# Token-major projections of a two-layer encoder: one matmul over 128 rows, or two over 64 rows into two PSUM banks

## The chip, the cores and the metric

The kernel runs on one core of a Trainium2 chip. The metric is the device time of one execution in microseconds, lower is better; the time before is the median of three runs.

## The reference

Two residual layers over 256 tokens of 2048 features, all in float32. Layer 0 mixes tokens by grouped-query attention (16 query heads, 4 key heads, RMS-norm of each head, rotary positions), layer 1 by a recurrent block (input projection, convolution of width 4, two gated linear recurrences, a GeLU gate, output projection). Each layer then has a feed-forward part with 5632 hidden features:

```python
def swiglu(h, w_gate, w_up, w_down):
    return (jax.nn.silu(h @ w_gate) * (h @ w_up)) @ w_down

for i in range(DEPTH):
    h = rms_norm(x, norm_mix[i])
    mix = attention_mixer(h, ...) if i % N_MIXERS == 0 else recurrent_mixer(h, ...)
    x = x + mix
    x = x + swiglu(rms_norm(x, norm_ffn[i]), ffn_w_gate[i], ffn_w_up[i], ffn_w_down[i])
```

Nearly all arithmetic is in the products with weight matrices: query, key and value (2048 x 3072), attention output, recurrent input (2048 x 4096) and output, and gate, up and down of each feed-forward part.

## The kernel before

**Precision.** TensorE multiplies in fp32r, a float32 format of lower precision. Each float32 operand is kept as a pair: `hi`, its value rounded to fp32r, and `lo`, the rest. A product takes three matmuls: hi with hi, hi with lo, lo with hi.

**Weights.** Weights come from HBM in pieces of 512 KB ("halves", `raw`, 128 partitions x 1024), in a fixed order. `load_half` (lines 106 to 118) issues the DMA on SP's queue, casts the piece to `hi` on ACT (L116) and takes the rest `lo` on DVE (L117). `raw`, `hi` and `lo` have five buffers each, so loads and casts run ahead of the matmuls by up to five pieces.

**Two kinds of projection.** The feature-major ones (`project`, `project_sum`, `project_two`; L201 and L231 to L233) hold weights as the stationary operand and stream 256 tokens (or 512 columns, hi and lo of the tokens side by side). The token-major ones, `project_tokens` (lines 211 to 228, matmuls at L223), hold 128 tokens of an activation as the stationary operand (128 features on the rows of the array, 128 tokens on its columns) and stream 512 output features of the weights. A call makes one group of 512 output features for all 256 tokens: two sums of 128 tokens x 512 in two PSUM banks, over 12 or 16 feature tiles `k`, with three matmuls for each `k` and half of the tokens `a`. In the last piece the order is such that the sum of the first 128 tokens is done six matmuls before the other.

Token-major are the attention's output projection, the recurrent output projection, and gate, up and down of both feed-forward parts. `output` (lines 376 to 390) calls `project_tokens` for four column groups and adds each sum to the residual `x_tok` on DVE (L384); in the last feed-forward part it also stores the result (L386), the last column group in two halves. `ffn` (line 635) works through the hidden features in parts of 12, 16 and 16 tiles of 128. A unit of four tiles is a gate call, whose sums go through SiLU on ACT into `fg`, and an up call, whose sums are multiplied with `fg` on DVE into `fu` (L641); `turned` (line 344) transposes it on DVE and ACT into four feature-major tiles, and L645 and L646 make the operand pair `act` from each. Then the down projection of that part runs over its tiles, the newest four last.

**Norms.** After each column group of `output`, `Norm.add` takes the sum of squares of the residual and makes operand tiles `xg` of it. For the recurrent block `Norm.spread` puts the tokens' scale on a diagonal (`ndg`, L330) and spreads it with a small matmul (L336) that the rest of the input projection waits for.

**PSUM.** Two pools of four banks each: `ps_a` for the sums of projections (tag `acc`) and `ps_m` for everything small in attention, recurrence and norms (tag `pm`). A call of `project_tokens` takes two banks of `ps_a`, so the next call can start while the sums of the last are read.

**Order.** The order on PE is that of the program. Work of attention heads and recurrence blocks is put between the projections' matmuls by `later(delay, fn)` and `step()`: a function is called after so many steps. So the last heads' transposes, scores and values are issued inside the first call of the attention's output projection. On the other engines the framework orders the instructions.

Of the kernel before, what the change touches and what calls it, by code (L numbers as in the profile page):

```python
# [12 lines left out]
F32 = mybir.dt.float32  # L13
F32R = mybir.dt.float32r
AF = mybir.ActivationFunctionType
ALU = mybir.AluOpType
AX = mybir.AxisListType

P = 128
# [10 lines left out]
WIDE = 512  # L30
# [39 lines left out]
def trunk(ctx, tc, w, out):  # L70
    nc = tc.nc
    act, dve, pool, pe, sync = nc.scalar, nc.vector, nc.gpsimd, nc.tensor, nc.sync
# [7 lines left out]
    ps_m = ctx.enter_context(tc.tile_pool(name="ps_m", bufs=4, space=bass.MemoryType.PSUM))  # L80
# [5 lines left out]
    def nm(s):  # L86
        uid[0] += 1
        return f"{s}_{uid[0]}"
# [61 lines left out]
    def half():  # L150
        n = taken[0]
        taken[0] += 1
        if n == 0:
            load_x(0, 2)
            scale_x(0)
            return load_half(*order[n], 4, partial(load_x, 2, 2))
        if n == 1:
            scale_x(1)
            return load_half(*order[n], 2)
        if n < KT // 2:  # L160
            if n % 2 == 0:
                load_x(2 * n, 4)
            if n < KT // 2 - 1:
                scale_x(n)
        if n == KT // 2 - 2:
            scale_x(n + 1)
            load_tables()
        if n == KT // 2 + 2:
            tiles = load_half(*order[n])
            token_squares(1)  # L170
            return tiles
        return load_half(*order[n])
# [8 lines left out]
    def step():  # L181
        clock[0] += 1
        due = [i for i, (t, _) in enumerate(waiting) if t <= clock[0]]
        if due:
            waiting.pop(due[0])[1]()

    def flush():
        while waiting:
            waiting.pop(0)[1]()

    def new_acc():
        return ps_a.tile([P, 2 * S], F32, tag="acc", name=nm("acc"))
# [16 lines left out]


    def project_tokens(xs, ready=0, close=None):
        accs = [new_acc() for _ in range(2)]
        for k0 in range(0, len(xs), 2):
            if close is not None and k0 == ready:
                flush()
                close()
            half()
            hi, lo = (t.rearrange("p (k c) f -> p k (c f)", k=2) for t in newest["tiles"])
            end = k0 + 2 == len(xs)
            for k, a in ((0, 0), (1, 0), (0, 1), (1, 1)) if end else ((0, 0), (0, 1), (1, 0), (1, 1)):  # L220
                xh, xl = (xs[k0 + k][:, o + a * P : o + (a + 1) * P] for o in (0, S))
                for n, (x, wt) in enumerate(((xh, hi), (xh, lo), (xl, hi))):
                    pe.matmul(  # L223
                        accs[a], x, wt[:, k, :], start=(k0 + k == 0 and n == 0), stop=(end and k == 1 and n == 2)
                    )
                step()
                step()
        return accs

    def three(o, hi, lo, x, start, stop):  # L230
        pe.matmul(o, hi, x[:, :S], start=start, stop=False)  # L231
# [8 lines left out]
    def project_sum(xs):  # L240
        bank = new_acc()
        for k0 in range(0, len(xs), HALF):
            sums(bank[:, :S], half(), xs, k0)
        return bank[:, :S], bank[:, S:]


    def project_two(xs, late):
        banks = [new_acc() for _ in range(2)]
        for t in banks:
            sums(t[:, :S], half(), xs, 0)  # L250
        rest = [half() for _ in range(2)]
        n = len(xs) - HALF - late
        for t, wt in zip(banks, rest):
            sums(t[:, :S], wt[:n], xs, HALF)
        for t, wt in zip(banks, rest):
            sums(t[:, :S], wt[n:], xs, HALF + n)
            yield t[:, :S], t[:, S:]
# [101 lines left out]
    fp = []  # L359
# [16 lines left out]
    def output(xs, norm=None, end=False, ready=0, close=None):  # L376
        for c in range(NCOL):
            accs = project_tokens(xs, ready, None if c else close)
            for a, acc in enumerate(accs):
                n = 2 if end and c == NCOL - 1 else 1  # L380
                for i in range(n):
                    sl = slice(i * WIDE // n, (i + 1) * WIDE // n)
                    y = x_tok[:, a, c, sl]
                    dve.tensor_tensor(y, y, acc[:, sl], ALU.add)  # L384
                    if end:
                        sync.dma_start(out=out[:, a, c, sl], in_=y)  # L386
            if norm is not None:
                norm.add(c)
        if norm is not None:
            norm.finish()  # L390
# [70 lines left out]
    for chunk in KEY_TILES:  # L461
        wt = half()
# [172 lines left out]
    def ffn(norm, nxt):  # L635
        def unit():
            g, u = (fp[0].tile([P, 2, WIDE], F32, tag=t, name=nm(t), bufs=1) for t in ("fg", "fu"))
            for a, acc in enumerate(project_tokens(norm.xs)):
                table_act(g[:, a, :], acc, AF.Silu, scale=norm.rt[:, a : a + 1])
            for a, acc in enumerate(project_tokens(norm.xs)):  # L640
                dve.scalar_tensor_tensor(u[:, a, :], acc, norm.rt[:, a : a + 1], g[:, a, :], ALU.mult, ALU.mult)  # L641
            for f in turned(u):
                h = act_tile()
                hi, lo = (h[:, o : o + S].rearrange("p (q t) -> p q t", t=32) for o in (0, S))
                act.copy(hi, f)  # L645
                dve.tensor_tensor(lo, f, hi.bitcast(F32), ALU.subtract)  # L646
                yield h

        for p, n in enumerate(PARTS):
            hid = [h for _ in range(n // FOUR) for h in unit()]  # L650
            last = p == len(PARTS) - 1
            if last and nxt is not None:
                ln_exp_tables()
            output(hid, nxt if last else None, last and nxt is None)
# [108 lines left out]
    for b in range(-1, NBLK):  # L763
# [9 lines left out]
        if nxt:  # L773
            accs = (project_sum(nr.xs) for _ in range(2)) if blk else project_two(nr.xs, FOUR)
# [101 lines left out]
```

## Time and profile before

| | before |
|---|---|
| median of 3 runs (lowest to highest) | 2036.44 us (2036.38 to 2036.95) |
| span of the profiled execution, first to last instruction | 2034.8 us |
| PE busy / weight loads busy | 2021.0 / 1722.5 us |
| DVE / ACT / POOL busy | 1311.9 / 1157.2 / 168.6 us |
| matmuls | 10124 |
| moved by DMA | 386.02 MB, mean 190 GB/s |
| mean granted TensorE clock | 0.998 |

The table of times gives no separate time for the profiled execution: its span is 1.6 us under the median of the runs. In rows of the profile a group is given as line, engine, operation, result <- operands, shape, count, then busy time in us and mean duration of one in ns, then the idle time of the engine just ahead of these instructions and what ended it. PEld is the weight load of a matmul, which the profile lists apart from PE. Matmuls are pipelined, so their durations overlap and the step from start to start is the cost of one.

### The profile page before, as it was taken

How to read it: one execution, taken by the hardware profiler on the slowest of the kernel's cores; microseconds unless marked ns; L12 is line 12 of the kernel's file. 1: busy time of each engine (PE TensorE's matmuls, PEld its weight loads, DVE VectorE, ACT ScalarE, POOL GpSimd, SP SyncE). 2: the span in 40 equal slices, each digit the busy share in tenths (PEclk: the TensorE clock that was granted, in tenths of full speed). 3: DMA queues.
4: the chain of work that ended last, by engine and by line, in shares of the span. 5: the costliest groups of instructions: out<-in, count | busy, mean ns of one | idle time of the engine just before them, and what ended most of it. 6: DMA issues, size and time to landing. Idle time of an engine off the chain costs nothing.

```text
span 2034.8 us, 27445 instructions
## 1 busy us (share of the span) xinstructions
PE 2021.0 (99%) x10124; PEld 1722.5 (85%) x10124; DVE 1311.9 (64%) x1899; ACT 1157.2 (57%) x1776; POOL 168.6 (8%) x213
## 2 busy tenths in 40 slices
PE   9999999999999999999899999999999999999999
PEld 8898888888888888888799998888888888888887
DVE  7998765654665445667778987765555556555553
ACT  7665755544555345556689987755435554355442
POOL 1563000000000000000134330000000000000000
PEclk9999999999999999999999999999999999999999
DMA  8444565665666656666556555566666666666664
GB/s 319 157 135 145 186 202 193 186 203 191 187 197 197 195 195 193 186 199 196 188 165 188 187 157 194 180 205 197 190 194 195 193 190 196 196 189 195 197 202 129
DMA packets 108998, 386.02 MB, mean 190 GB/s; under 512 B 12224, under 2 KB 12992, under 8 KB 108736
## 3 DMA queue, kind: packets, MB, share of 16 engines
q1 hardware_dynamic: 108720, 384.26, 59.7%
q8 instruction: 79, 1.29, 0.3%
q14 instruction: 55, 0.45, 0.1%
q10 hardware_dynamic: 144, 0.02, 0.0%
HBM read 382.13 MB, written 2.10 MB: 189 GB/s over the span
## 4 chain that ended last, share of the span: by engine, by line
PE 54%; issue 40%; DVE 2%; DMA 2%; ACT 1%; POOL 0%; SPq 0%; DVEq 0%; POOLq 0%
PE acc L223 40%; PE acc L201 3%; PE acc L231 3%; PE acc L232 3%; PE acc L233 3%; PE pm L232 1%; PE pm L233 1%; PE pm L231 1%; DVE lo L117 1%; DMA x_tok<-in_xt_dram 1%; DMA graw<-in_w_gates_dram 0%; DMA raw<-in_w_k_dram 0%; PE pm L576 0%; DMA raw<-in_w_qv_dram 0%; ACT hi L116 0%
## 5 line engine op out<-in xcount | busy, mean ns | idle before, releaser
L117 DVE TENSOR_TENSOR lo<-raw,hi 128x1024 fp32r<-128x1024 f32 (+1 forms) x708 | 868.7, 1230 | 665.5 <-ACT hi L116 657.1
L116 ACT CAST hi<-raw 128x1024 fp32r<-128x1024 f32 (+1 forms) x708 | 739.4, 1047 | 751.7 <-PE acc L223 744.0
L223 PE MATMUL acc<-hi,xg 128*128 128x512 f32 x2816 | 867.8, 389 | 0.0
L223 PEld LDWEIGHTS acc<-hi,xg 128*128 128x128 f32 x2816 | 528.6, 188 | 109.6
L223 PE MATMUL acc<-hi,act 128*128 128x512 f32 x1920 | 594.2, 389 | 0.0
L223 PE MATMUL acc<-lo,xg 128*128 128x512 f32 x1408 | 547.7, 389 | 0.0
L223 PEld LDWEIGHTS acc<-hi,act 128*128 128x128 f32 x1920 | 360.4, 188 | 74.4
L223 PE MATMUL acc<-lo,act 128*128 128x512 f32 x960 | 373.5, 389 | 0.0
L223 PEld LDWEIGHTS acc<-lo,xg 128*128 128x128 f32 x1408 | 264.3, 188 | 54.9
L223 PEld LDWEIGHTS acc<-lo,act 128*128 128x128 f32 x960 | 180.2, 188 | 37.1
L231 PE MATMUL acc<-xg,hi 128*128 128x256 f32 x512 | 145.0, 283 | 0.0
L232 PE MATMUL acc<-xg,hi 128*128 128x256 f32 x512 | 145.0, 283 | 0.0
L233 PE MATMUL acc<-xg,lo 128*128 128x256 f32 x512 | 144.7, 283 | 0.0
L201 PE MATMUL acc<-xg,hi 128*128 128x512 f32 x384 | 125.8, 396 | 0.2 <-ACT hi L116 0.2
L354 ACT COPY tf<-tb 32x256 f32<-32x256 f32 x272 | 109.8, 404 | 3.7 <-DVE tb L348 0.2
L231 PEld LDWEIGHTS acc<-xg,hi 128*128 128x128 f32 x512 | 98.3, 192 | 0.0
L232 PEld LDWEIGHTS acc<-xg,hi 128*128 128x128 f32 x512 | 98.2, 192 | 0.1
L233 PEld LDWEIGHTS acc<-xg,lo 128*128 128x128 f32 x512 | 98.2, 192 | 0.0
L201 PEld LDWEIGHTS acc<-xg,lo 128*128 128x128 f32 x384 | 71.8, 188 | 16.0 <-DVE lo L117 1.9
L201 PE MATMUL acc<-xg,lo 128*128 128x256 f32 x384 | 84.8, 288 | 0.5 <-DVE lo L117 0.4
L356 DVE COPY tf<-tb 32x256 f32<-32x256 f32 x272 | 77.2, 284 | 4.0
L667 POOL MEMSET cb<- 128x2 f32 x16 | 1.7, 108 | 823.1 <-PE acc L233 811.6
(172 smaller groups left out, 1324.5 us busy)
## 6 DMA issues: line engine op xcount, KB each, us to landing
raw<-in_w_gate_dram SPq DMA_DIRECT2D x176, 512.0 KB, 4.0
raw<-in_w_up_dram SPq DMA_DIRECT2D x176, 512.0 KB, 3.9
raw<-in_w_down_dram SPq DMA_DIRECT2D x176, 512.0 KB, 3.8
raw<-in_w_in_dram SPq DMA_DIRECT2D x64, 512.0 KB, 4.3
raw<-in_w_qv_dram SPq DMA_DIRECT2D x40, 512.0 KB, 4.2
raw<-in_w_o_dram SPq DMA_DIRECT2D x32, 512.0 KB, 3.6
raw<-in_w_out_dram SPq DMA_DIRECT2D x32, 512.0 KB, 4.0
graw<-in_w_gates_dram SPq DMA_DIRECT2D x32, 256.0 KB, 3.4
```

What stands on the lines that cost most here:

```text
L116: newest["cast"] = act.copy(hi[:, sl, :], raw[:, sl, :])
L117: dve.tensor_tensor(lo[:, sl, :], raw[:, sl, :], hi[:, sl, :].bitcast(F32), ALU.subtract)
L201: pe.matmul(o, w, x, start=(k == 0 and not part), stop=(k == total - 1 and not part))
L223: pe.matmul(accs[a], x, wt[:, k, :], start=(k0 + k == 0 and n == 0), stop=(end and k == 1 and n == 2))
L231: pe.matmul(o, hi, x[:, :S], start=start, stop=False)
L232: pe.matmul(o, hi, x[:, S:], start=False, stop=False)
L233: pe.matmul(o, lo, x[:, :S], start=False, stop=stop)
L354: act.copy(o, y)
L356: dve.tensor_copy(o, y)
L667: pool.memset(b[:, 0:2], 0.0)
```

## The change

In `project_tokens` each matmul is split by the rows of the array. The first 64 rows (features) are multiplied at row position 0 with the sum in a bank of `ps_a`, the other 64 at row position 64 with the sum in a bank of `ps_m`. The two matmuls follow each other in the program. When all of a call's matmuls are issued, `joined` copies the second sum to SBUF on ACT and adds the first to it on DVE; the readers (SiLU, the product with `fg`, the residual add) then read that tile in SBUF.

```diff
     def project_tokens(xs, ready=0, close=None):
-        accs = [new_acc() for _ in range(2)]
+        accs = [(new_acc(), ps_m.tile([P, WIDE], F32, tag="pm", name=nm("pm"))) for _ in range(2)]
...
                 for n, (x, wt) in enumerate(((xh, hi), (xh, lo), (xl, hi))):
-                    pe.matmul(
-                        accs[a], x, wt[:, k, :], start=(k0 + k == 0 and n == 0), stop=(end and k == 1 and n == 2)
-                    )
+                    first, last = k0 + k == 0 and n == 0, end and k == 1 and n == 2
+                    for r in range(2):
+                        rows = slice(r * P // 2, (r + 1) * P // 2)
+                        pe.matmul(
+                            accs[a][r], x[rows], wt[rows, k, :],
+                            start=first, stop=last, tile_position=(r * P // 2, 0),
+                        )
                 step()
                 step()
-        return accs
+        return [joined(pair) for pair in accs]
+
+    def joined(pair):
+        t = fp[0].tile([P, WIDE], F32, tag="join", name=nm("join"), bufs=3)
+        act.copy(t, pair[1])
+        dve.tensor_tensor(t, pair[0], t, ALU.add)
+        return t
```

## The prediction

> **What bounds the kernel now.** I read the page first, then the busy time by stage, then the groups of the one line that is edited, and last the instruction rows on which that line's rate shows.
>
> ```profile
> PE 2021.0 (99%) x10124; PEld 1722.5 (85%) x10124; DVE 1311.9 (64%) x1899; ACT 1157.2 (57%) x1776; POOL 168.6 (8%) x213
> ...
> PE 54%; issue 40%; DVE 2%; DMA 2%; ACT 1%; POOL 0%; SPq 0%; DVEq 0%; POOLq 0%
> ...
> L223 PE MATMUL acc<-hi,xg 128*128 128x512 f32 x2816 | 867.8, 389 | 0.0
> L223 PEld LDWEIGHTS acc<-hi,xg 128*128 128x128 f32 x2816 | 528.6, 188 | 109.6
> L223 PE MATMUL acc<-hi,act 128*128 128x512 f32 x1920 | 594.2, 389 | 0.0
> L223 PE MATMUL acc<-lo,xg 128*128 128x512 f32 x1408 | 547.7, 389 | 0.0
> ...
> L223 PE MATMUL acc<-lo,act 128*128 128x512 f32 x960 | 373.5, 389 | 0.0
> ```
>
> The matmul engine is busy for 99% of the span, and the edited line, L223, has 2816 + 1920 + 1408 + 960 = 7104 of its 10124 matmuls, with no idle time ahead of any group. The busy time by stage (columns: window, length, then PE, PEld, DVE, ACT, POOL with counts, clock, DMA share, GB/s) says where they lie:
>
> ```profile
> 174.60:190.00 15.40, 15.06 (x82) 12.38 (x80) 13.21 (x37) 9.39 (x27) 1.87 (x4) 1.00 0.42 138
> 190.00:985.80 795.80, 795.80 (x3519) 659.14 (x3517) 480.24 (x629) 414.63 (x564) 0.00 (x0) 1.00 0.62 193
> 985.80:1225.80 240.00, 233.15 (x1926) 231.97 (x1925) 191.26 (x323) 207.44 (x355) 84.65 (x110) 0.99 0.55 175
> 1225.80:2031.00 805.20, 805.20 (x3553) 666.59 (x3551) 470.25 (x583) 403.92 (x531) 0.20 (x1) 1.00 0.61 191
> ```
>
> Windows 2 and 4 are token-major projections and nothing else: PE has no gap in 1601 us, while DVE, ACT and the DMA engines stand at 50 to 62%. The casts on ACT even wait for PE, not the other way round:
>
> ```profile
> ACT hi L116 <- PE acc L223: 744.0, 479, 2.4
> ```
>
> So this part costs (matmuls) x (time from one start to the next). That step comes from one piece of the chain that ended last, all 3552 matmuls of layer 1, and from the timeline of PE and of its weight loads:
>
> ```profile
> 1225.85 805.16 PE acc L223 x3552
> ```
>
> ```profile
> 699.98 0.62 PE L223 MATMUL acc<-hi,act 128*128 128x512 f32 x2
> 700.43 0.39 PE L223 MATMUL acc<-lo,act 128*128 128x512 f32 x1
> ...
> 699.98 0.19 PEld L223 LDWEIGHTS acc<-hi,act 128*128 128x128 f32 x1
> 700.21 0.19 PEld L223 LDWEIGHTS acc<-lo,act 128*128 128x128 f32 x1
> ```
>
> 805.16 / 3552 = 226.7 ns. A matmul is recorded as 389 ns, so two are in the array at once; the load of the next weights starts as a matmul starts and lies wholly beside it (188 < 226.7). The rest of the kernel isn't edited.
>
> **The change, part by part.** *The matmuls.* Each of the 7104 becomes two, each over 64 rows with the same 512 columns, at row positions 0 and 64, into two banks. 14208 matmuls and 14208 loads take the place of 7104 and 7104. What counts is the time of a pair, against 226.7 ns. No row of this trace shows a matmul over 64 rows, so I bound it.
>
> Upper bound: the halves run one after the other, each streaming 512 columns at the old step: 2 x 226.7 = 453.3 ns. Lower bound: the fixed part of a step vanishes. Matmuls with half the columns show that part:
>
> ```profile
> 1149.77 0.28 PE L231 MATMUL acc<-xg,hi 128*128 128x256 f32 x1
> ...
> 1152.89 0.28 PE L233 MATMUL acc<-xg,lo 128*128 128x256 f32 x1
> ```
>
> 26 steps lie between these two rows: 3.12 / 26 = 120.0 ns for 256 columns. 226.7 - 120.0 = 106.7 ns for the other 256, so 512 columns stream in 213.3 ns and 13.3 ns of each step is fixed. A pair can't be shorter than 213.3 ns, as each half must stream its 512 columns.
>
> Between them stand the two loads of a pair. The smallest steps of a load and its matmul are these, the four transposes of the chain and four loads of the norm's small matmul, then six 256-column matmuls:
>
> ```profile
> 107.49 0.44 PE pm L576 x4
> ...
> 997.71 0.52 PEld L336 LDWEIGHTS pm<-ndg,ones 128*128 128x128 f32 x4 [2.48 <-issue]
> ...
> 177.77 0.28 PE L231 MATMUL pm<-kv,qs 128*128 128x256 f32 x1
> ...
> 178.45 0.40 PE L223 MATMUL acc<-hi,act 128*128 128x512 f32 x1
> ```
>
> 0.44 / 4 = 110 ns; (0.52 - 0.19) / 3 = 110 ns; (178.45 - 177.77) / 6 = 113 ns. If loads of the two halves run one behind the other, a pair needs 220 ns by the first, 227 by the last, and 240 by the long stream of 120.0 ns.
>
> I take 226.7 ns, no change: each half of the array goes on at its own old step, with the 13.3 ns at each change of weights, the halves run beside each other, and two loads of 110 to 113 ns just fit (220 to 227). This is nearest to the row of 3552, which has the same columns, the same precision and the same changes of weights. That the halves overlap is the assumption here; what the trace gives for it is that the array already holds two matmuls and a load at the same time, and that the halves share neither rows nor a bank. [...]
>
> *The joins.* Each of the 152 sums (44 gate, 44 up, 64 output) gets an ACT copy out of PSUM and a DVE add ahead of its old reader.
>
> ```profile
> L401 ACT ACTIVATE fg<-acc,nr 128x512 f32<-128x512 f32 x44 | 30.2, 690 | 19.5 <-PE acc L223 19.5
> ...
> L261 ACT COPY hy<-acc 128x256 f32<-128x256 f32 x24 | 8.8, 370 | 11.9 <-PE acc L201 11.9
> ...
> L384 DVE TENSOR_TENSOR x_tok<-x_tok,acc 128x512 f32<-128x512 f32 x62 | 39.6, 680 | 0.0
> ```
>
> The copy lies between 370 ns (half the width) and 690 ns (full width with a scale), say 620; the add has L384's shape, 680. That is 152 x 0.62 = 94 us on ACT and 152 x 0.68 = 103 us on DVE, spread over 1617 us: DVE goes from 60% to about 66% of window 2, ACT from 52% to 58%. Behind the copies stand casts in ACT's queue, which now wait for PE 1.6 us each time (744.0 / 479), so this is hidden. Without that cover it would be 197 us. The extra banks come from the pool that only the attention and recurrence stages use, and four sums of two banks fill both pools twice over, so the next call still has its own banks.
>
> Exposed are the places where PE or the end waits for the newest sum. The end:
>
> ```profile
> 2030.61 0.39 PE L223 MATMUL acc<-hi,act 128*128 128x512 f32 x1
> 2031.03 0.75 DVE L384 TENSOR_TENSOR x_tok<-x_tok,acc 128x256 f32<-128x256 f32 x2 [0.61 <-PE acc L223]
> ```
>
> The last adds follow the last matmul at once; copy and add come between: +1.3 us. The step from layer 0 to the recurrence, where PE already waits for a chain on DVE that begins with the output adds:
>
> ```profile
> 985.51 1.28 DVE L384 TENSOR_TENSOR x_tok<-x_tok,acc 128x512 f32<-128x512 f32 x2
> ...
> 997.74 0.68 PE L336 MATMUL pm<-ndg,ones 128*128 128x128 f32 x4 [2.31 <-DVE ndg L330]
> ```
>
> All that lengthens this chain is lost: two adds of 0.68, +1.4 us. The first down projection of each layer (12 tiles), whose last four operands come from the newest up projection:
>
> ```profile
> L223 PE MATMUL acc<-hi,xg x2816: 389/389/389, 267.7 to 1943.6; 128*128 128x512 f32 x188
> ```
>
> ```profile
> 407.85 1.43 DVE L646 TENSOR_TENSOR act<-tf,act 128x256 fp32r<-128x256 f32 x4
> ```
>
> The first gate projection starts at 267.7; three units of two calls of 96 matmuls end 576 x 0.2267 = 130.6 us later, at 398.3. The ninth operand's low part is wanted 50 matmuls after that, at 409.6, and it is ready at about 408.3 (the first of these four): 1.3 us to spare. Copy and add bring 1.3 us, and up to 2.7 where both sums queue up: 0 to 1.4 us lost, twice; I take +1.4 in all. Projections of 16 tiles start their last four operands 24 matmuls (5.4 us) later and lose nothing.
>
> *The switches.* In the first call of the attention's output projection nine bursts of ordinary 128-row matmuls of the last heads stand between the projection's, and the trace shows them next to L223 with no gap. Such a burst now changes the tiling twice. If each change waits for the matmul in flight to leave, it costs up to 389 - 227 = 162 ns: 18 x 0 to 0.16 = 0 to 2.9 us; I take the middle, +1.5.
>
> *Sum.* 1.3 + 1.4 + 1.4 + 1.5 = 5.6 us, and nothing for the pairs. The profiled execution spans 2034.8 us; the median of the three runs is 2036.4, so 1.6 us lie outside the span, which I leave as they are. 2036.4 + 5.6 = 2042.0. With the spread of these terms (the tail alone to all at their upper ends: 1.3 + 2.7 + 2.8 + 2.9 = 9.7, and some more for a late sum elsewhere) this case reaches from 2037 to 2049. About 0.2% (4 us) is what a measurement of this kernel can tell from no change.
>
> **The rivals.** *The fixed part hides (the other side: faster).* While one half of the array changes weights the other streams, so the 13.3 ns stop being lost. It decides if they belong to the step as a whole and not to each half. For it: six 256-column matmuls ran at 113 ns a step and not 120, so the fixed part can be smaller. Against it: in 3552 steps it never was, and each half still changes its weights at each of its matmuls. The pair then takes 213.3 to 220 ns: 7104 x (-13.3 to -6.7) = -95 to -47 us, with the 5.6 us 1947 to 1995, middle 1971.
>
> *The loads are the bound.* Each load waits for the start of the matmul ahead of it, as in every row above, and its own matmul starts 113 to 120 ns after it, whatever the other half does. For it: the long stream of 256-column matmuls, the weight-load row of window 3 (231.97 of 240.00 us busy), steps at 120.0. Against it: loads of the same 188 to 190 ns ran at 110. It decides from 113.3 ns a load. At 116.7 to 120 the pair takes 233 to 240 ns: 7104 x (6.7 to 13.3) = +47 to +95 us, 2089 to 2137.
>
> *Each half waits for its own load.* If a load can't run beside a matmul of the same rows, a half streams, then loads, then streams: 226.7 + 110 = 337 ns; 7104 x 0.110 = +781 us, 2823. The rows above speak against it: every load lies beside a matmul of the same 128 rows. [...]
>
> *No overlap.* The change doesn't do what it says, the second half starts when the first has streamed: 7104 x 226.7 ns = +1610 us, 3652. For it: no step above is shorter than 110 ns, and nothing shows two matmuls that start together; against it, no two matmuls here left each other's rows free.
>
> **How the numbers follow.** Chances: no change in the pair (2042) 0.34; the fixed part hides (1971) 0.20; loads the bound (2113) 0.26; each half waits for its load (2823) 0.07; no overlap (3652) 0.13. The first is the likeliest, since 220 to 227 ns of loads fit into a step that 3552 matmuls keep. The range takes in the first three, 0.80, from 1947 to 2140. Faster by over 0.2% is the hidden fixed part, 0.20. Within 0.2% is the low end of the first case, 0.05. Slower has the rest, 0.29 + 0.26 + 0.07 + 0.13 = 0.75.
>
> **What would show it.** In windows of the feed-forward stages the profile of the changed kernel should have some 882 matmuls in 100 us where it now has 441 (1 / 0.2267), with two starts close to each other or about 113 ns apart. Over 900 means a hidden fixed part; 833 to 858 means the loads; 594 the wait for its own load; 441 no overlap. DVE should have 152 adds of about 0.68 us and ACT 152 copies of 0.6; PE idle ahead of the norm's small matmul should grow from 2.31 to about 3.7 us, and the last adds should start 1.3 us later after the last matmul than the 0.03 us of now. PE gaps inside the feed-forward stages, on the joins or on banks, would make the argument on the cover wrong.

## The result and the profile after

The changed kernel takes 2045.92 us (median of 3 runs, 2045.44 to 2049.33) against 2036.44 us: 1.005 times the time before, 95% interval 1.003 to 1.007. It is slower by 9.5 us; forecast were 5.6 us, that is 2042.0 us.

The engine totals of the changed kernel:

```profile
PE 2030.5 (99%) x17228; PEld 1764.2 (86%) x17228; DVE 1413.1 (69%) x2051; ACT 1227.5 (60%) x1928; POOL 166.8 (8%) x213
```

17228 matmuls are 10124 + 7104, so every edited matmul became two, and PE's busy time grew by 9.5 us only. The groups show it: each old group is there twice, once for each bank, and the two busy times (863.8 and 863.6 us) lie on top of each other.

```profile
L226 PE MATMUL acc<-hi,xg 64*128 64x512 f32 x2816 | 863.8, 386 | 0.0
L226 PE MATMUL pm<-hi,xg 64*128 64x512 f32 x2816 | 863.6, 386 | 0.0
...
L236 ACT COPY join<-pm 128x512 f32<-128x512 f32 x152 | 88.6, 583 | 66.9 <-PE pm L226 66.9
...
L237 DVE TENSOR_TENSOR join<-acc,join 128x512 f32<-128x512 f32 x152 | 103.5, 681 | 45.2 <-ACT join L236 45.2
```

The timeline of PE and of its loads in layer 0's feed-forward part (start, duration, engine, line, operation):

```profile
702.05 0.39 PE L226 MATMUL acc<-lo,act 64*128 64x512 f32 x1
702.06 0.39 PE L226 MATMUL pm<-lo,act 64*128 64x512 f32 x1
702.06 0.18 PEld L226 LDWEIGHTS acc<-hi,act 64*128 64x128 f32 x1
702.06 0.18 PEld L226 LDWEIGHTS pm<-hi,act 64*128 64x128 f32 x1
702.28 0.39 PE L226 MATMUL acc<-hi,act 64*128 64x512 f32 x1
702.28 0.39 PE L226 MATMUL pm<-hi,act 64*128 64x512 f32 x1
```

Both matmuls of a pair start within 10 ns of each other, so do both loads, and the next pair comes 0.23 us later. So the pairs cost nothing, and the 9.5 us must lie elsewhere. Stages from the first matmul of one to the first of the next, first before, then changed (columns as in the prediction's table by stage):

```profile
174.60:267.70 93.10, 92.76 (x429) 76.93 (x428) 70.50 (x140) 57.25 (x104) 1.87 (x4) 1.00 0.56 181
267.70:985.80 718.10, 718.10 (x3169) 594.59 (x3168) 422.95 (x526) 366.76 (x486) 0.00 (x0) 1.00 0.62 193
985.80:1225.70 239.90, 233.05 (x1926) 231.88 (x1925) 191.26 (x323) 207.34 (x355) 84.55 (x110) 0.99 0.55 175
1225.70:1312.80 87.10, 87.10 (x387) 72.13 (x386) 65.81 (x103) 60.61 (x98) 0.30 (x1) 1.00 0.61 199
1312.80:2030.60 717.80, 717.80 (x3168) 594.56 (x3167) 404.44 (x481) 343.41 (x433) 0.00 (x0) 1.00 0.61 190
```

```profile
174.50:270.70 96.20, 95.89 (x813) 76.66 (x814) 76.10 (x146) 60.60 (x111) 1.89 (x4) 1.00 0.52 170
270.70:988.90 718.20, 718.20 (x6339) 593.31 (x6335) 466.88 (x594) 397.85 (x554) 0.00 (x0) 1.00 0.62 194
988.90:1232.50 243.60, 237.10 (x1928) 235.24 (x1926) 192.71 (x325) 206.77 (x355) 82.72 (x109) 0.97 0.54 174
1232.50:1324.10 91.60, 89.37 (x771) 75.20 (x772) 71.12 (x110) 65.25 (x106) 1.72 (x2) 0.98 0.55 183
1324.10:2042.00 717.90, 717.90 (x6338) 631.26 (x6334) 447.23 (x548) 375.01 (x501) 0.00 (x0) 1.00 0.61 191
```

The two long feed-forward stages, 6336 of the 7104 pairs, are as long as before (718.2 against 718.1 us, 717.9 against 717.8), with twice the matmuls. The loss lies in the three short stages between them and at the end. This profiled execution is the slowest of the three runs; 3.1 us more than in a repeated run (a1, below) lie in the recurrent output projection, so a1's profile, not this one, stands for the median.

### The profile page after: what moved, and what is told of

Read it like the earlier page. It is cut to its first block, busy times and chain, and to the rows that moved or that the text cites. A ratio compares the mean times of both kernels' runs of the same rounds, so it can differ in the third digit from the quotient of the medians.

```text
span 2047.5 us, 41954 instructions
## 1 busy us (share of the span) xinstructions
PE 2030.5 (99%) x17228; PEld 1764.2 (86%) x17228; DVE 1413.1 (69%) x2051; ACT 1227.5 (60%) x1928; POOL 166.8 (8%) x213
## 4 chain that ended last, share of the span: by engine, by line
PE 54%; issue 40%; DVE 2%; ACT 2%; DMA 1%; POOL 0%; SPq 0%; DVEq 0%; POOLq 0%; ACTq 0%
PE pm L226 26%; PE acc L226 12%; PE acc L201 5%; PE acc L241 2%; PE acc L242 2%; PE acc L243 2%; PE pm L242 1%; DVE lo L117 1%; PE pm L243 1%; PE pm L241 1%; DMA graw<-in_w_gates_dram 0%; ACT hi L116 0%; ACT sg L411 0%; DMA raw<-in_w_k_dram 0%; ACT L411 0%
## 5 line engine op out<-in xcount | busy, mean ns | idle before, releaser
L226 PE MATMUL acc<-hi,xg 64*128 64x512 f32 x2816 | 863.8, 386 | 0.0
L226 PE MATMUL pm<-hi,xg 64*128 64x512 f32 x2816 | 863.6, 386 | 0.0
L226 PE MATMUL acc<-hi,act 64*128 64x512 f32 x1920 | 593.8, 387 | 1.4 <-ACT hi L116 1.4
L226 PE MATMUL pm<-hi,act 64*128 64x512 f32 x1920 | 593.7, 387 | 0.0
L226 PEld LDWEIGHTS acc<-hi,xg 64*128 64x128 f32 x2816 | 518.1, 184 | 68.0
L226 PE MATMUL acc<-lo,xg 64*128 64x512 f32 x1408 | 543.5, 386 | 0.0
L226 PE MATMUL pm<-lo,xg 64*128 64x512 f32 x1408 | 543.5, 386 | 0.0
L226 PEld LDWEIGHTS pm<-hi,xg 64*128 64x128 f32 x2816 | 518.1, 184 | 26.6
L226 PE MATMUL acc<-lo,act 64*128 64x512 f32 x960 | 371.4, 387 | 0.8 <-DVE lo L117 0.8
L226 PE MATMUL pm<-lo,act 64*128 64x512 f32 x960 | 371.4, 387 | 0.0
L226 PEld LDWEIGHTS pm<-lo,xg 64*128 64x128 f32 x1408 | 259.1, 184 | 13.3
```

Of the source, the lines that this page charges most:

```text
L226: pe.matmul(accs[a][r], x[rows], wt[rows, k, :], start=first, stop=last, tile_position=(r * P // 2, 0),)
```

## The experiments

The table gives, for each kernel, by how many us each stage of its profiled execution is longer than before's (FFN 0 and FFN 1 are the feed-forward parts of the two layers). f2, whose pairs themselves are slower, is not in it. The profiled executions took 1.7 to 2.0 us more than their spans.

| kernel | median us (runs) | attention output projection | FFN 0 | recurrence | recurrent output projection | FFN 1 | end |
|---|---|---|---|---|---|---|---|
| changed, first profile | 2045.92 (3) | 3.1 | 0.1 | 3.7 | 4.5 | 0.1 | 1.3 |
| changed, again (a1) | 2045.23 (5) | 3.2 | 0.1 | 3.5 | 1.4 | 0.0 | 1.4 |
| b1, first calls whole | 2041.92 (10) | 0.3 | 0.0 | 3.6 | 0.2 | 0.1 | 1.4 |
| c1, one cast back in place | 2044.30 (5) | 3.1 | 0.1 | 3.5 | 1.0 | 0.0 | 1.4 |
| d1, two banks and joins, no split | 2047.43 (5) | 3.7 | 1.5 | 2.6 | -0.1 | 1.7 | 1.3 |
| e1, first half of the rows only | 2040.44 (1) | 2.7 | 0.1 | 1.2 | 0.0 | 0.1 | 0.0 |
| g1, split without joins | 2045.28 (1) | 3.1 | 0.1 | 1.9 | 2.9 | 0.0 | 0.0 |
| f1, halves three by three | 2049.2 (1) | 3.2 | 0.4 | 2.5 | 4.2 | 0.7 | 1.4 |
| h1, changed with waits filled | 2046.68 (5) | 3.1 | 0.1 | 3.7 | 1.7 | 0.1 | 1.4 |
| h2, before with one wait filled | 2034.86 (11) | 0.1 | 0.0 | -1.6 | -0.1 | 0.1 | -0.1 |
| h3, before with two waits filled | 2035.15 (11) | 0.1 | -0.1 | -1.7 | -0.1 | 0.1 | 0.0 |

**a1: the changed kernel again.** No edit.

> The changed kernel as it is, for a finer time and a second profile. Theory S (single places): the pairs cost nothing, and the loss sits in four places, as the first profile has them: 3.0 us where ordinary matmuls stand between split ones in the attention's output projection, 1.5 us more at the step to the recurrence, 2.2 us of idle PE early in the recurrent output projection, 1.4 us at the end. Then the time is again 2045 to 2047, and the 2.2 us are there again; the 3.4 us by which the first profiled execution is over the two others are a lower TensorE clock behind that idle time, and come and go. Theory P (pairs): the loss is spread over the 7104 pairs, 1.3 ns each; then the starts of the feed-forward windows drift apart from those of before evenly.

Measured: 2045.23 us (2044.61 to 2049.57), 1.0045 times before, interval 1.0033 to 1.0058. Its span is 2044.2, 9.4 us more than before's, and its stages sum to that: 3.2 + 0.1 + 3.5 + 1.4 + 1.4 = 9.6, less 0.2 ahead of the first stage. The idle time in the recurrent output projection is not 2.2 us again, as expected, but 0.8, and the recurrence loses 3.5 us, not 1.5.

**e1: one half alone.** The matmuls of rows 64 to 127 are left out, and with them the second bank and the join, so the sums cover only the first 64 features of each tile.

```diff
-                    for r in range(2):
+                    for r in range(1):
...
-        return [joined(pair) for pair in accs]
+        return [pair[0] for pair in accs]
```

> Only the matmuls of the first 64 rows are issued, into one bank, without a join; the second half of each sum is left out. The step of a lone 64-row matmul. If the 13.3 ns that a step has over the streaming of its 512 columns belong to each half of the array, as the forecast took it, the step stays at 226.7 ns and the span is 2035 to 2042. If they belong to 128 rows or to the step as a whole, it is 213 to 220 ns and the span 1940 to 1990.

Measured: 2040.44 us. PE's timeline:

```profile
699.77 0.61 PE L226 MATMUL acc<-hi,act 64*128 64x512 f32 x2
...
701.13 0.61 PE L226 MATMUL acc<-hi,act 64*128 64x512 f32 x2
```

From the first row to the last lie six matmuls (two in the first row, four in the rows left out): 1.36 / 6 = 226.7 ns each. A lone 64-row matmul has the step of a 128-row one and of a pair. So what a step has beyond streaming (13.3 ns by the prediction's estimate) belongs to each half, and nothing of it hides beside the other half.

**f1 and f2: how far apart the halves can be issued.** f1 issues three matmuls of one half, then three of the other; f2 issues twelve and twelve (all of a weight piece).

```diff
 # f1
-                for n, (x, wt) in enumerate(((xh, hi), (xh, lo), (xl, hi))):
-                    for r in range(2):
+                for r in range(2):
+                    for n, (x, wt) in enumerate(((xh, hi), (xh, lo), (xl, hi))):
 # f2: the loop over r also outside the loop over (k, a)
```

> The same split matmuls in another order: for each feature tile and half of the tokens first the three at row position 0, then the three at row position 64. If PE starts matmuls only in the order of the program, and a busy half holds up what comes behind, three and three overlap in one place alone: four steps for three pairs, 302 ns a pair, 2045 + 7104 x 0.0756 = 2582 us. If a waiting matmul lets those of the other half pass, the time stays near 2045.

> As three by three, but for each weight piece first all twelve matmuls at row position 0, then the twelve at row position 64 (the small attention work then comes between pieces). Three by three cost nothing: the two halves ran as two streams of their own, 0.1 us apart. If a half can run ahead past any number of waiting matmuls of the other, the step stays at 226.7 ns a pair and the time is 2045 to 2050. If it can pass only a few, the halves take turns for part of each piece; with no passing at all twelve pairs take 22 steps and not 12: 2045 + 7104 x 0.189 = 3388 us. A value between says how far it sees.

Measured: f1 2049.2 us, f2 2755.29. In f1 the feed-forward stages lose 0.4 and 0.7 us: the halves run as two streams, in layer 0 half a step apart, each at 0.23 us. In f2 they take turns:

```profile
900.66 0.39 PE L227 MATMUL acc<-hi,act 64*128 64x512 f32 x1
900.67 0.49 PE L227 MATMUL pm<-hi,act 64*128 64x512 f32 x1
...
901.34 0.39 PE L227 MATMUL acc<-hi,act 64*128 64x512 f32 x1
...
904.58 0.49 PE L227 MATMUL pm<-hi,act 64*128 64x512 f32 x1
```

The first `pm` matmul starts at 900.67, beside the fourth from last of the twelve `acc` matmuls, and ahead of three that come before it in the program (the last of them at 901.34). The next turn of `pm` starts at 904.58. Twelve pairs thus take 904.58 - 900.67 = 3.91 us, 326 ns a pair; 7104 x (326 - 226.7) = 705 us, and f2 is 710 us slower than a1. So here a matmul for idle rows passed three waiting matmuls of the other half; with twelve in a row it did not pass more. Issued pair by pair, as in the change, no half has to get that far ahead.

**b1: the first calls not split.** The first call of each output projection, between whose matmuls the attention heads and recurrence blocks are issued, keeps 128-row matmuls, one bank and no join.

```diff
+        whole = close is not None
...
+                    if whole:
+                        pe.matmul(accs[a][0], x, wt[:, k, :], start=first, stop=last)
+                        continue
...
-        return [joined(pair) for pair in accs]
+        return [pair[0] if whole else joined(pair) for pair in accs]
```

> The first of the four calls of both mixers' output projections is done with whole 128-row matmuls, one bank a sum and no join; the other 74 calls stay split. Theory S: the ordinary matmuls then stand between ordinary ones, so the 3.0 us go, and the cast that had moved behind four table operations on ACT is back in its place, so the 2.2 us of idle PE go as well (with or without the low clock behind it): 2039 to 2041, the first gate matmul at 267.7 us and not 270.7. Theory P: 2 of 76 calls are 2.6 percent of the loss, 0.25 us: 2045.7.

Measured: 2041.92 us, 1.0024 times before (1.0014 to 1.0033), 0.9 us over the expectation's upper end. The attention output projection loses 0.3 us instead of 3.2, the recurrent one 0.2 instead of 1.4. PE's timeline at one of the nine bursts, before and changed:

```profile
176.42 0.39 PE L223 MATMUL acc<-hi,act 128*128 128x512 f32 x1
176.65 0.60 PE L576 MATMUL pm<-ident,pr 128*128 128x128 f32 x4
177.00 0.47 PE L223 MATMUL acc<-hi,act 128*128 128x512 f32 x1
177.31 0.39 PE L223 MATMUL acc<-lo,act 128*128 128x512 f32 x1
```

```profile
176.42 0.39 PE L226 MATMUL acc<-hi,act 64*128 64x512 f32 x1
...
176.74 0.66 PE L586 MATMUL pm<-ident,pr 128*128 128x128 f32 x4
177.32 0.49 PE L226 MATMUL acc<-hi,act 64*128 64x512 f32 x1
...
177.66 0.39 PE L226 MATMUL acc<-lo,act 64*128 64x512 f32 x1
```

From the projection's last matmul ahead of the burst to its next one it was 0.58 us and is 0.90, and the step behind that was 0.31 us and is 0.34: some 0.35 us for two changes of tile shape. e1, which has neither joins nor second banks, still loses 2.7 us in this stage: it is the change of tile shape that costs, 2.7 to 3.1 us over 18 changes, 0.15 to 0.17 us each. In the groups it shows as no idle time, only in the starts. That the matmul in flight has to leave first, as the prediction's estimate has it, is not shown: the burst starts at 176.74, before the recorded end (176.42 + 0.39 = 176.81, a modelled time) of the matmul ahead of it.

**d1: joins and banks without the split.** 128-row matmuls, even tiles `k` into one bank and odd ones into the other, with the changed kernel's joins.

```diff
-                    for r in range(2):
-                        rows = slice(r * P // 2, (r + 1) * P // 2)
-                        pe.matmul(accs[a][r], x[rows], wt[rows, k, :], ...)
+                    pe.matmul(accs[a][k], x, wt[:, k, :], start=(k0 == 0 and n == 0), stop=(end and n == 2))
```

> Whole 128-row matmuls, as many as before, but the sums of even and odd feature tiles go to two banks and are joined as in the change: the joins and the banks alone, without the split. Theory S: the end costs 1.4 us and the step to the recurrence 1.5 us, no switches and no moved cast: 2039 to 2040. If the joins or the banks are what costs, 2045 to 2046; if the split alone costs, 2036.5.

Measured: 2047.43 us, 1.0052 times before (1.0039 to 1.0064), 8 us over what I expected. Its bursts cost what they cost before, but its waits are others than those of the changed kernel (what waited, on which line, for what; us in total, times, longest):

```profile
PE pm L554 <- DVE mx L567: 2.5, 1, 2.5
```

In the attention output projection a transpose waits 2.5 us for a bank of `ps_m`, of which the call holds two of four; the changed kernel holds as many, and its waits there are 0.2 us or less. In each layer the first down projection waits 1.0 us for its operands (`act`, L651 and L652), most of the 1.5 and 1.7 us of the table. So joins can cost at these places. That it depends on the order on ACT and DVE, which the framework chose otherwise here, is likely but not shown. d1 therefore isolates no cost of the changed kernel but one, the chain ahead of the norm's matmul, below.

**g1: the split without joins.** The sums in the second bank are computed but left out of the results.

```diff
-        return [joined(pair) for pair in accs]
+        return [pair[0] for pair in accs]
```

> All split matmuls and both banks, but no copy and no add: the readers take the first bank alone, the second half of each sum is left out. If the joins make the loss at the end and the longer chain ahead of the recurrence, 1.4 us go at the end and 1.6 to 2.3 us in the recurrence, while the 3.1 us in the attention's output projection (switches) and the idle time at the moved cast (0.8 us or more) stay: span 2039.5 to 2042. If the second bank alone makes the losses, the span stays at 2044.

Measured: 2045.28 us, a span of 2043.5 us, 1.5 us above the expectation's upper end. By the span alone the rival (the second bank, 2044) would look right; the stages say otherwise. As expected the end costs nothing and the recurrence loses 1.9 us instead of 3.5. But the recurrent output projection loses 2.9 us, 1.5 more than in a1.

**c1: one cast back in place.** In the recurrent output projection PE waits for a piece of weights. On ACT the sixth piece's cast stood between the last block's square roots before, and stands behind the GeLU and two table loads in a1, f1 and g1. c1 makes the third square root follow that cast.

```diff
+            if taken[0] == 414 and "sqrt" in newest:
+                follow(newest["sqrt"], newest["cast"])
```

> The changed kernel, with one more rule for the order on ACT: the third square root of the last recurrence block comes after the cast of the sixth weight piece of the recurrent output projection, which is where that cast stood before the change. Theory S: PE's 2.2 us of idle time there go and nothing else does: 2043 to 2044, or up to 4.5 us off where the low clock had followed. If the wait there is for something else than this cast (the block's last operands, a bank), the time stays at 2046.

Measured: 2044.30 us (2043.53 to 2046.11) and 1.0 us lost in that stage against a1's 1.4. The intervals of the two kernels overlap: inconclusive. In c1's trace the cast is back in its place, but the five casts behind the table loads start 14.2 us after the projection's first matmul (12.8 before), and PE still waits 0.6 us, now for a `lo` piece. So the place of this one cast is not the whole cause.

**h1: the changed kernel with waits filled.** The recurrence of the changed kernel has three short PE waits ahead of the longest one. h1 puts small matmuls, whose results nobody reads, into the waits.

```diff
+    def fill(n):
+        t = ps_m.tile([P, P], F32, tag="pm", name=nm("pm"))
+        for _ in range(n):
+            pe.matmul(t, ones, ones, start=True, stop=True)
 # fill(12) ahead of the late half in project_two, fill(4) in the norm's
 # spread, fill(14) ahead of the first block's first gates
```

> The changed kernel, with small matmuls of a constant tile (results unused) put on PE where it waits in the step to the recurrence: 12 before the late half of the first input projections, 4 before the norm's small matmul, 14 before the first gate matmuls (0.22 us each). Theory C (clock): of the 3.5 us that the change loses in the recurrence none is more idle time (6.6 us against 6.85), it is a second spell at half clock behind a thinner first wait; with PE kept busy both spells go (6.84 us of clock), and the time is 2045.2 - 6.8 = 2038 to 2040. Theory L (longer chain): the joins lengthen the chain of DVE steps that PE waits for, filling the wait changes nothing or costs a little: 2045 to 2046.

Measured: 2046.68 us (2045.56 to 2047.01), no gain. Windows of a1 and of h1 (clock is the third number from the end):

```profile
1001.00:1008.00 7.00, 6.30 (x32) 6.01 (x31) 1.88 (x9) 2.60 (x5) 1.74 (x6) 0.54 0.44 150
...
1017.00:1025.00 8.00, 6.74 (x32) 6.54 (x33) 3.68 (x8) 4.51 (x7) 1.54 (x3) 0.57 0.59 184
```

```profile
1001.00:1008.00 7.00, 6.83 (x57) 6.64 (x56) 2.40 (x10) 2.15 (x4) 1.49 (x5) 1.00 0.45 151
...
1017.00:1025.00 8.00, 6.17 (x29) 5.88 (x30) 3.95 (x8) 3.83 (x7) 1.95 (x6) 0.57 0.44 135
```

The half clock of the first window is gone, and 57 matmul records stand where there were 32 (8 of the 57 are fills). Yet PE's last wait for the convolution ends no earlier (rows of a1, then of h1):

```profile
1017.17 0.38 PE L241 MATMUL pm<-xs,ghi 128*128 128x256 f32 x1 [1.56 <-DVE xs L278]
1018.64 0.58 PE L242 MATMUL pm<-xs,ghi 128*128 128x256 f32 x1 [1.09 <-DVE xs L279]
```

```profile
1018.69 0.58 PE L241 MATMUL pm<-xs,ghi 128*128 128x256 f32 x1 [2.44 <-DVE xs L284]
```

h1's row is the matmul that stands at 1017.17 in a1, so DVE hands over its operand 1.5 us later, and PE only arrives earlier at a wait that DVE ends. And the half clock at that wait, the second window, is still there.

**h2 and h3: the kernel before with its waits filled.** h2 has fill(14) ahead of the first gates; h3 also has fill(10) in the norm's spread, and fill(18) at the first place.

> The kernel before, with 14 such matmuls before the first gate matmuls only. Theory C: its one spell at half clock (3.4 us) goes: 2033 to 2034. Theory L: no change, 2036.9, or some tenths more.

> The kernel before, with constant matmuls in both waits of the step to the recurrence: 10 before the norm's small matmul (2.2 us of a 2.3 us wait) and 18 before the first gate matmuls. With 14 at the second place alone one spell at half clock went and a new one of 1.7 us came behind the first wait. If the clock follows how little PE does over some us, this one goes too: 2032.5 to 2034. If filling the first wait delays the chain, 2035 to 2037.

Measured: 2034.86 us (2034.58 to 2037.01) and 2035.15 us (2034.61 to 2036.62), both 0.9992 times before, interval 0.9983 to 1.0001. The same window of before and of h2, there with the filled wait:

```profile
1009.00:1017.00 8.00, 5.40 (x23) 4.64 (x24) 6.37 (x14) 2.35 (x4) 1.42 (x5) 0.57 0.69 230
```

```profile
1009.00:1017.00 8.00, 7.06 (x61) 6.86 (x60) 6.03 (x13) 3.50 (x6) 1.91 (x5) 1.00 0.68 224
```

With the wait filled the clock stays at 1.00 behind it, and the recurrence is 1.6 us shorter in h2's profile, 1.7 in h3's. Behind the earlier wait, ahead of the norm's small matmul, h2 has a stretch at half clock that before has not (row in the last section); h3, which fills that wait too, has none. But the interval just includes no change, both medians lie above the upper end of what the clock theory expected (2034), and h3 adds nothing to h2.

## Why the prediction was right in its forecast, and where its sum was off

**The pairs: right.** The step stayed at 226.7 ns, which by itself refutes the hidden fixed part; e1 adds that a lone half has the same step. The loads as the bound are refuted by two loads that start together (both at 702.06 us). That also answers one reason given for the forecast: the loads of a pair do not follow each other at 110 to 113 ns, so the 220 to 227 ns that just fit played no part. The wait for the half's own load is refuted by loads that lie beside matmuls of the same rows (0.18 us from 702.06, beside matmuls of 0.39 us from 702.05 and 702.06). No overlap at all is refuted by every pair (in the rows shown the two start 17 ns apart or less), and f2 shows when part of it would come true (326 ns a pair with twelve of one half in a row).

**The joins beside PE: right.** The copies took 583 ns and the adds 681 (forecast 620 and 680), and the feed-forward stages kept their length.

**The end: right,** 1.4 us for 1.3. The last copy and add stand between the last matmul and the last residual add (changed kernel's timeline):

```profile
2041.95 0.39 PE L226 MATMUL acc<-hi,act 64*128 64x512 f32 x1
2042.38 0.58 ACT L236 COPY join<-pm 128x512 f32<-128x512 f32 x1 [0.77 <-PE pm L226]
2043.05 0.68 DVE L237 TENSOR_TENSOR join<-acc,join 128x512 f32<-128x512 f32 x1
2043.76 0.76 DVE L394 TENSOR_TENSOR x_tok<-x_tok,join 128x256 f32<-128x256 f32 x2
```

**The switches: mis-sized.** 2.7 to 3.1 us against 1.5: I took the middle of 0 to 0.16 us per change, and the measured 0.15 to 0.17 lie at its upper end. The reason for the bound, that the matmul in flight has to leave, was my estimate, and no run shows it; what the runs show is a cost of 0.15 to 0.17 us a change. The choice of the middle had no row behind it.

**The step to the recurrence: right as far as it went, then cut short.** The norm's small matmul starts 997.74 - 985.8 = 11.9 us into the stage before, and later in the changed kernel (a1's timeline):

```profile
1002.41 1.22 PE L346 MATMUL pm<-ndg,ones 128*128 128x128 f32 x4 [0.70 <-DVE ndg L340]
```

1002.41 - 988.9 = 13.5 us, +1.6 for a forecast 1.4. It is 13.4 in d1 (joins, no split) and 11.8 and 11.9 in e1 and g1 (split, no joins): the joins alone make it. The wait itself did not grow to 3.7 us, as I had said, but split into three (1.45, 0.86 and this 0.70 us). The failed step is that I ended the sum at this matmul. PE's last wait of the chain ends at

```profile
1013.33 0.58 PE L232 MATMUL pm<-xs,ghi 128*128 128x256 f32 x1 [0.89 <-DVE xs L269]
```

before, 27.5 us into the stage, and at 1018.64 in a1, 29.7: +2.2. Without joins it ends 27.8 (e1) and 27.2 us (g1) into the stage, so these 2.2 us go with the joins.

Behind it PE runs at half clock (256-column matmuls 0.21 us apart instead of 0.12). The stretch at half clock is as long in both kernels, 6.8 us (a window of before, then of a1):

```profile
1009.67:1016.47 6.80, 4.51 (x17) 3.93 (x18) 5.70 (x12) 1.74 (x3) 0.89 (x5) 0.50 0.73 243
```

```profile
1017.74:1024.54 6.80, 5.90 (x27) 5.90 (x28) 2.94 (x7) 3.48 (x6) 1.54 (x3) 0.50 0.56 178
```

But before it begins 3.7 us ahead of the end of the last wait, and 2.3 us of it are waits anyway; in a1 it begins 0.9 us ahead of it. So 3.1 us of it lie behind the wait before and 5.9 in a1. Half of such time counted as lost, my estimate from the clock of 0.50, makes +1.4, and 2.2 + 1.4 = 3.6 for the 3.5 measured (by the steps, 0.12 us instead of 0.21, it is 0.43 of that time: +1.2 and 3.4). This second part is a matter of where the stretch happens to fall, not a fixed price of the change: in f1, with the same joins, the last wait also ends 29.7 us into the stage, but only 3.8 us at half clock lie behind it, and the stage loses 2.5 us. In e1, without joins, 5.0 us lie behind it: 0.3 + 0.9 = 1.2 us, as in the table. h1 shows that taking away the first stretch at half clock (1000.7 to 1007.5 in a1) gains nothing.

**The first down projections: wrong.** Forecast +1.4 in all, measured 0.1. The 1.3 us to spare held. That the mechanism exists is shown by d1 (1.5 and 1.7 us), so the estimate was on the edge; what decided is not shown.

**The recurrent output projection: not forecast.** +1.4 us in a1, +4.5 in the first profile. There PE waits for one piece of weights (waits and a window of the changed kernel's first profile):

```profile
PE acc L226 <- ACT hi L116: 1.4, 1, 1.4
PE acc L226 <- DVE lo L117: 0.8, 1, 0.8
```

```profile
1250.00:1254.00 4.00, 4.00 (x26) 3.21 (x24) 4.00 (x4) 2.02 (x3) 0.00 (x0) 0.66 0.78 261
```

The idle 2.2 us are followed by a stretch at clock 0.66, and the stage loses 4.5 us, more than its idle time; a1 idles 0.8 us there, its clock stays at 1.00, and it loses 1.4 us. b1 removes the loss, g1 without joins does not: it comes with the first call in two halves and two banks, for e1 (one half, one bank) and d1 (two banks, no split) lose nothing here (0.0 and -0.1). The cast that moved on ACT is the candidate: it is moved in every kernel that loses 1.4 us or more here (the changed kernel, a1, g1, f1, h1) and in its place in those that lose 0.2 or less (b1, d1, e1). But c1 puts it back and still loses 1.0, so the cause is not settled, and what moves the cast is open. My argument that the casts run 1.6 us ahead held in the feed-forward stages, on which it was made, and not here, where ACT also does the recurrence's table work.

The forecast total came within 4 us partly by luck: a term of 1.4 that did not come stood against three that were too small or missing (1.6, 2.1 and 1.4 us in a1). The forecast that carried the result is the one on the pairs.

## What to carry to other kernels

Splitting a matmul that already fills all 128 rows into two row tiles gained nothing here (512 columns, fp32r): each tile kept the full step of 226.7 ns, and the join and the changes of tile shape were pure cost. If row tiles are used, issue the halves alternately, and keep other tile shapes out of the loop: a change cost 0.15 to 0.17 us of PE time that no wait in the profile shows. When a change adds work to a chain that PE waits for, follow it to the last wait of the stage, look where the half clock falls, and read each stage's slack on ACT and DVE in that stage.

## What the runs showed of the hardware

- The two row tiles ran as two streams. In layer 1 of the first profile the half at row 64 leads its partner by 17 ns, though it comes second in the program (1600.39 against 1600.41 us); in a1 it follows by up to 10 ns (1600.50 against 1600.49 us).
- In f2 a stream went on past three waiting matmuls of the other half (from 900.67 us); twelve in a row made a pair 326 ns instead of 226.7.
- The half clock came in stretches of 3.41 us, one or two in a row: two from 1009.67 us in before; two from 1000.14, two from 1017.21 and one from 1249.31 in the first profile. The three starts of the first profile lie on one grid of 3.41 us, 17.07 and 232.10 us apart, which are 5 and 68 steps; in a1 the stretches start at 1000.66 and 1017.73, also five steps apart. Cut by that grid, PE's waits in the 3.41 us ahead of the half clock add up to 2.26 us in before and to 1.99, 2.47 and 2.23 us in the first profile; 1.74 us in before (the first row below) were not followed by half clock. A first stretch at half clock with 2.03 us of waits (before) or 0.86 and 0.97 us (first profile) was followed by a second one; the second ones (0.25, 0 and 0 us) and the single one (0 us) were followed by full clock. These are single stretches of this one program; no run set out to test them.
- In a1 the stretch ahead of the half clock, from 997.25, has two short waits, of 1.45 and 0.86 us. The wait of 2.3 us ahead of the norm's small matmul is cut in two before (0.57 and 1.74 us), and the clock stays at 1.00; in h2 it falls into one stretch, and the next is at half clock. Windows on the grid, of before, then of h2; 3.41 less the first time behind the length is the wait:

```profile
996.00:999.41 3.41, 1.67 (x14) 1.70 (x15) 1.69 (x6) 0.00 (x0) 0.07 (x3) 1.00 0.83 258
```

```profile
994.36:997.77 3.41, 1.11 (x8) 0.89 (x8) 3.19 (x9) 1.20 (x3) 0.20 (x4) 1.00 0.62 190
997.78:1001.17 3.39, 3.39 (x17) 3.39 (x17) 0.00 (x0) 0.62 (x1) 1.19 (x1) 0.50 0.71 262
```
